# Moving the byte places of the streamed halves and of the low weights in a two-layer encoder

## The chip, the cores and the metric

The kernel runs on one core of one Trainium2 chip. The metric is the device time of one launch in microseconds; the kernel before takes 2561.47 us, the median of three runs (2561.24 to 2562.99). TensorE multiplies matrices: it holds a block of weights (the stationary operand) and streams the columns of the other operand past it, both read from SBUF, the on-chip memory, and adds into PSUM. VectorE and ScalarE do elementwise work, GpSimd a little, and SyncE's queue issues the loads of weights.

## The reference

A trunk of two layers over 272 tokens (16 learned tokens and 256 of input) of 2048 channels, in float32:

```python
for i in range(DEPTH):
    h = _rmsnorm(h_stream, norm_mix[i])
    proj = h @ w_in[i]                       # q, k, v, f, two gates
    ...                                      # attention: 8 heads over 2 key/value heads, rotary
    a_br = attn @ w_attn_br[i]
    ...                                      # fourier: real part of a 2-D DFT of f
    s_br = fr.reshape(B, L, FOURIER_WIDTH) @ w_four[i]
    merged = g_attn * a_br + g_four * s_br
    h_stream = h_stream + merged @ w_out[i]
    h2 = _rmsnorm(h_stream, norm_ffn[i])
    up = h2 @ w_up[i]                        # 2 x 5632 columns
    u_gate = _dwconv3_centred(up[..., :D_FF], w_conv[i], b_conv[i])
    u_val = up[..., D_FF:]
    h_stream = h_stream + (jax.nn.silu(u_gate) * u_val) @ w_down[i]
return h_stream[:, N_META:]
```

## The kernel before

Everything is kept transposed: channels on the 128 partitions, tokens along the row. A matrix product is done in three matmuls on numbers cut in two: a float32 value is a high half (the value rounded to the matmul's type, float32r) and a low half (what the rounding left). High weights times high half, high weights times low half and low weights times high half are added up in one PSUM tile; low times low is left out.

Weights come in chunks of 4 blocks of 128 rows by 256 columns (`CW` = 4, `MG` = 2). SyncE's queue loads a chunk into `raw`, ScalarE casts it into `wh` (L193), VectorE subtracts to get `wl` (L196); both are tiles of 4096 bytes a partition with three buffers each. A written list, `order`, gives the sequence of the groups of matmuls; `group` works through one of them. For each block of 128 rows and each of two output blocks it issues

```python
nc.tensor.matmul(o, h[:, c, sl], a, start=kt == 0, stop=False)    # L248: high weights, high half
nc.tensor.matmul(o, h[:, c, sl], b, start=False, stop=False)      # L249: high weights, low half
nc.tensor.matmul(o, lo[:, c, sl], a, start=False, stop=kt == nk - 1)  # L250: low weights, high half
```

or, where twice the width fits in a PSUM tile, the first two as one matmul over both halves (L244) and then the third (L245). Every matmul has its own weight load (LDWEIGHTS) ahead of it.

The groups are named f, k, v, q (inputs of the two branches), ga and gf (gates), s and a (branch outputs), o (the output product), ug and uv (the two halves of the up product) and d (the down product). f, k, v, q, ga, gf, ug and uv stream from `xHL`, which holds both halves of the scaled residual side by side; d streams from `gHL`; a from `qH` and `qL`; o from `mH` and `mL`. The row of each half has room for `XP` = 320 columns of 4 bytes (1280 bytes, five times 256), so that the 272 tokens can begin at a chosen column: `X_AT`, `Q_AT` and `G_AT` hold that column for layer 0 and layer 1.

Layer 0 works on all 272 tokens. Layer 1 drops columns whose results are not used: f, k and v take 272, then q, ga, gf, a, o and ug take 258 (from token 14) and uv and d take 256 (from token 16). There the two halves together fit 512 columns, so uv and d run as pairs of a 512 and a 256 column matmul; the last of d's groups runs as three of 256.

The order on each engine is the order in which the program is written; `split_w` is called a little ahead of its use by `pump`.

Of the kernel before, what the change touches and what calls it, by code (L numbers as in the profile page):

```python
# [10 lines left out]
F32 = mybir.dt.float32  # L11
F32R = mybir.dt.float32r
# [4 lines left out]
P = 128  # L17
# [3 lines left out]
T = NM + SEQ  # L21
# [3 lines left out]
NH = 8  # L25
# [7 lines left out]
CW = 4  # L33
MG = 2
FF_SPLIT = (24, 20)
PRE = 26
XP = 320
# [11 lines left out]
TH = T // 2 + 2  # L49
X_AT, Q_AT, G_AT = (8, 24), (24, 40), (40, 48)  # L50
BLK = ((0, 16), (16, 144), (144, 272))
# [60 lines left out]
def encoder_kernel(ctx, tc, xT, params, consts, bmat, w_in, w_abr, w_four, w_f64, w_out, w_up, w_down, outT):  # L112
# [7 lines left out]
    order = []  # L120
# [26 lines left out]
    chunks = [ch for _, chs in order for ch in chs]  # L147
    folded = {i for i, k in enumerate(k for k, chs in order for _ in chs) if k[1] == "s"}
    st = {"raw": 0, "fetch": 0, "next": 0, "grp": 0}
    raws, splits, behind = {}, {}, {}  # L150
# [36 lines left out]
    def split_w(i, a, b, eng=None):  # L187
        if i not in splits:
            splits[i] = tuple(wp.tile([P, CW, MG * P], F32R, tag=t, name=f"{t}{i}") for t in ("wh", "wl"))
        h, lo = splits[i]  # L190
        r = raws[i]
        if eng is None:
            nc.scalar.copy(h[:, a:b], r[:, a:b])  # L193
        else:
            eng.tensor_copy(h[:, a:b], r[:, a:b])
        nc.vector.tensor_tensor(lo[:, a:b], r[:, a:b], h[:, a:b].bitcast(F32), op=ALU.subtract)  # L196
        if b == CW:
            del raws[i]
# [187 lines left out]
    def xs(k, half, lo=0, l=0):  # L386
        return xHL[:, k, half, X_AT[l] + lo:X_AT[l] + T]

# [60 lines left out]
    for l in range(DEPTH):  # L449
# [7 lines left out]
        with tc.tile_pool(name=f"mix{l}", bufs=1) as mp:  # L457
            x64 = mp.tile([96, TH], F32R, name="x64")
            E = mp.tile([P, NH, XP], F32, tag="q1", name="E")[:, :, 0:T]
            qL = mp.tile([P, NH, XP], F32R, name="qL")[:, :, Q_AT[l]:Q_AT[l] + T]  # L460
            AHn = 3 * 4 * T
# [236 lines left out]
            for pn in pns:  # L698
                nc.gpsimd.memset(pn[:, 0:P], 0.0)
            qH = mp.tile([P, NH, XP], F32R, tag="q1", name="qH")[:, :, Q_AT[l]:Q_AT[l] + T]  # L700

# [149 lines left out]
            for half in range(2):  # L851
                mH = mL = None
                for kind, i in BRANCH_ORDER[half]:
# [19 lines left out]
                    else:  # L873
                        if mH is None:
                            drain()
                            mHf = mp.tile([P, AHn], F32R, tag="aH", name="mH")
                            mLf = mp.tile([P, ALn], F32R, tag="aL", name="mL")
                            mH, mL = (t_[:, :8 * XP].rearrange("p (k t) -> p k t", k=8)[:, :, Q_AT[l]:Q_AT[l] + T] for t_ in (mHf, mLf))
                        ps = group((l, "a", i), lambda kt: (qH[:, kt, lo:T], qL[:, kt, lo:T]), W)
# [16 lines left out]
        with tc.tile_pool(name=f"ffn{l}", bufs=1) as fp:  # L896
            hold = {}
            push(norm_stats(hold), 8)
            fused = 2 * W2 <= 512
            k0 = 0  # L900
            for c, n in enumerate(FF_SPLIT):
                gHL = fp.tile([P, FF_SPLIT[0], 2, XP], F32R, tag="gHL", name="gHL")[:, :, :, G_AT[l]:G_AT[l] + T]
                gH, gL = gHL[:, :, 0, :], gHL[:, :, 1, :]
                for i in range(k0 // MG, (k0 + n) // MG):
# [3 lines left out]
                    for m in range(MG):  # L908
# [12 lines left out]
                        cs.append(cv)  # L921
                    ps = group((l, "uv", i), (lambda kt: (xHL[:, kt, :, X_AT[l] + lo2:X_AT[l] + T],)) if fused else xr(lo2), W2)
                    for m in range(MG):
# [12 lines left out]
                for mg in range(8):  # L936
                    two = fused and not (lastc and mg == 7)
                    ps = group((l, "d", c, mg), (lambda kt: (gHL[:, kt, :, lo2:T],)) if two
                               else (lambda kt: (gH[:, kt, lo2:T], gL[:, kt, lo2:T])), W2)
# [64 lines left out]
```

## Time and profile before

| | |
|---|---|
| median of three runs | 2561.47 us |
| the profiled execution's own time | 2561.68 us |
| its span, first to last instruction | 2559.8 us |
| TensorE busy | 2552.6 us, 19732 matmuls |
| weight loads busy | 2494.2 us |
| VectorE, ScalarE busy | 1690.4 us, 1211.4 us |
| mean granted TensorE clock | 0.999 |

In the rows, PE is a matmul and PEld a weight load, DVE is VectorE, ACT is ScalarE. A row of the groups by shape gives the source line, the engine, output<-inputs by tile name, the shape, how many there were (x), then busy time and the mean duration of one in ns. Durations of successive matmuls overlap: one is shown some 280 ns long while the next begins some 120 ns after it began. A row of a window gives its limits, its length, then the busy time and count of each engine's instructions, and after these the granted clock, the share of the DMA engines and what they moved. A row of the timeline gives the start in us and the duration. A row of the waits gives the engine and line that waited, for whom, the total in us, the number of times and the longest.

### The profile page before, as it was taken

Reading aid. Unit: us, or ns where it says so; the run is one execution under the profiler, and the core shown is the slowest. Engines: PE = TensorE matmul, PEld = TensorE weight load, DVE = VectorE, ACT = ScalarE, POOL = GpSimd, SP = SyncE. Lnnn points to the kernel's source line nnn. Section 1 sums busy time; section 2 is a strip of 40 time slices with the busy share of each in tenths; the row PEclk is TensorE's granted clock in tenths of the full one; section 3 lists DMA queues with packets and bytes.
Section 4 is the critical chain, followed back from the end, with each engine's and each line's share of the span. In section 5 each row is a group of like instructions: output and inputs, shape, how many; then the busy total and the mean of one; then the engine's idle time right before and its main releaser. Section 6 shows DMA issues by size and latency. Waiting matters only on the chain.

```text
span 2559.8 us, 47859 instructions
## 1 busy us (share of the span) xinstructions
PE 2552.6 (100%) x19732; PEld 2494.2 (97%) x19732; DVE 1690.4 (66%) x2691; ACT 1211.4 (47%) x1741; POOL 18.3 (1%) x37
## 2 busy tenths in 40 slices
PE   9999999999999999999999999999999999999999
PEld 9999999999999999999999999999999998999988
DVE  7687767766565446655566878677766665566654
ACT  6455434554444334444444555345554543455443
POOL 0000000000000000000000000000000000000000
PEclk9999999999999999999999999999999999999999
DMA  7555656555555555555554546666555556655565
GB/s 236 166 153 166 192 183 189 185 175 179 180 176 181 177 178 181 175 181 178 177 172 153 174 150 199 192 199 191 184 186 189 185 187 190 189 188 186 186 202 160
DMA packets 132011, 465.34 MB, mean 182 GB/s; under 512 B 15312, under 2 KB 19280, under 8 KB 131792
## 3 DMA queue, kind: packets, MB, share of 16 engines
q1 hardware_dynamic: 127424, 457.37, 56.5%
q10 hardware_dynamic: 4368, 4.92, 0.6%
q8 instruction: 154, 2.52, 0.4%
q14 instruction: 65, 0.53, 0.1%
HBM read 457.35 MB, written 2.10 MB: 179 GB/s over the span
## 4 chain that ended last, share of the span: by engine, by line
PE 98%; DVE 1%; DMA 0%; ACT 0%; issue 0%; SPq 0%; DVEq 0%; ACTq 0%
PE ps_ug L249 7%; PE ps_ug L248 7%; PE ps_ug L250 7%; PE ps_uv L244 6%; PE ps_d L244 6%; PE ps_d L249 4%; PE ps_d L250 4%; PE ps_d L248 4%; PE ps_uv L248 3%; PE ps_uv L249 3%; PE ps_uv L250 3%; PE ps_uv L245 3%; PE ps_d L245 3%; PE ps_o L249 2%; PE ps_o L248 2%; PE ps_gf L248 2%
## 5 line engine op out<-in xcount | busy, mean ns | idle before, releaser
L196 DVE TENSOR_TENSOR wl<-raw,wh 128x1024 fp32r<-128x1024 f32 (+1 forms) x835 | 1016.8, 1220 | 697.3 <-ACT wh L193 692.4
L193 ACT CAST wh<-raw 128x1024 fp32r<-128x1024 f32 (+1 forms) x834 | 871.3, 1047 | 994.4 <-PE ps_ug L249 159.5
L248 PE MATMUL ps_ug<-xHL,wh 128*128 128x272 f32 (+1 forms) x1408 | 399.6, 284 | 0.0
L249 PE MATMUL ps_ug<-xHL,wh 128*128 128x272 f32 (+1 forms) x1408 | 399.0, 283 | 0.0
L250 PE MATMUL ps_ug<-xHL,wl 128*128 128x272 f32 (+1 forms) x1408 | 399.0, 283 | 0.0
L248 PEld LDWEIGHTS ps_ug<-xHL,wh 128*128 128x128 f32 x1408 | 264.2, 188 | 0.9
L249 PEld LDWEIGHTS ps_ug<-xHL,wh 128*128 128x128 f32 x1408 | 264.2, 188 | 0.1
L250 PEld LDWEIGHTS ps_ug<-xHL,wl 128*128 128x128 f32 x1408 | 264.1, 188 | 0.0
L244 PE MATMUL ps_uv<-xHL,wh 128*128 128x512 f32 x704 | 245.0, 390 | 0.0
L244 PE MATMUL ps_d<-gHL,wh 128*128 128x512 f32 x664 | 230.3, 391 | 0.0
L249 PE MATMUL ps_d<-gHL,wh 128*128 128x272 f32 (+1 forms) x744 | 212.0, 285 | 0.0
L248 PE MATMUL ps_d<-gHL,wh 128*128 128x272 f32 (+1 forms) x744 | 212.0, 285 | 0.0
L250 PE MATMUL ps_d<-gHL,wl 128*128 128x272 f32 (+1 forms) x744 | 212.0, 285 | 0.0
L248 PE MATMUL ps_uv<-xHL,wh 128*128 128x272 f32 x704 | 200.6, 285 | 0.0
L249 PE MATMUL ps_uv<-xHL,wh 128*128 128x272 f32 x704 | 200.6, 285 | 0.0
L250 PE MATMUL ps_uv<-xHL,wl 128*128 128x272 f32 x704 | 200.6, 285 | 0.0
L245 PE MATMUL ps_uv<-xHL,wl 128*128 128x256 f32 x704 | 198.5, 282 | 0.0
L245 PE MATMUL ps_d<-gHL,wl 128*128 128x256 f32 x664 | 185.9, 280 | 0.0
L244 PEld LDWEIGHTS ps_uv<-xHL,wh 128*128 128x128 f32 x704 | 132.1, 188 | 26.9
L244 PEld LDWEIGHTS ps_d<-gHL,wh 128*128 128x128 f32 x664 | 124.2, 187 | 27.2
L248 PE MATMUL ps_ga<-xHL,wh 128*128 128x272 f32 (+1 forms) x512 | 147.5, 288 | 0.0
L248 PE MATMUL ps_gf<-xHL,wh 128*128 128x272 f32 (+1 forms) x512 | 146.3, 286 | 0.0
(284 smaller groups left out, 5891.7 us busy)
## 6 DMA issues: line engine op xcount, KB each, us to landing
raw<-in_w_up SPq DMA_DIRECT2D x352, 512.0 KB, 3.5
raw<-in_w_in SPq DMA_DIRECT2D x207, 512.0 KB, 3.6
raw<-in_w_down SPq DMA_DIRECT2D x176, 512.0 KB, 3.5
raw<-in_w_out SPq DMA_DIRECT2D x64, 512.0 KB, 3.5
raw<-in_w_four SPq DMA_DIRECT2D x32, 512.0 KB, 3.7
raw<-in_w_abr SPq DMA_DIRECT2D x32, 512.0 KB, 3.5
qs<-qp ACTq DMA_DIRECT2D x32, 68.0 KB, 4.1
outT<-ot ACTq DMA_DIRECT2D x16, 128.0 KB, 4.0
```

Source lines behind the costliest of these rows:

```text
L193: nc.scalar.copy(h[:, a:b], r[:, a:b])
L196: nc.vector.tensor_tensor(lo[:, a:b], r[:, a:b], h[:, a:b].bitcast(F32), op=ALU.subtract)
L244: nc.tensor.matmul(o2, h[:, c, sl], ab, start=kt == 0, stop=False)
L245: nc.tensor.matmul(o, lo[:, c, sl], ab[:, 0, :], start=False, stop=kt == nk - 1)
L248: nc.tensor.matmul(o, h[:, c, sl], a, start=kt == 0, stop=False)
L249: nc.tensor.matmul(o, h[:, c, sl], b, start=False, stop=False)
L250: nc.tensor.matmul(o, lo[:, c, sl], a, start=False, stop=kt == nk - 1)
```

## The change

The change gives each half its own first column, and lets the low weights of a chunk begin at a place inside a longer tile (`WL_AT`, in columns of 4 bytes, by layer and kind of group; 0 where none is named). A tile of 32 columns that nothing uses (`shift`) moves the tiles behind it by 128 bytes. Where both halves are streamed by one matmul, the function `both` builds a view whose step between the halves is 320 columns plus the difference of the two places.

With the addresses that the built programs give to the tiles, the operands begin at these bytes, counted mod 256:

| groups | columns | high half | low half | high weights | low weights |
|---|---|---|---|---|---|
| layer 0: f, k, v, q, ga, gf, ug, uv, d | 272 | 32 -> 176 | 32 -> 48 | 128 | 128 -> 192 |
| layer 0: a, o | 272 | 32 -> 240 | 32 -> 80 | 128 | 128 -> 64 |
| layer 1: f, k, v | 272 | 96 | 96 -> 128 | 128 | 128 |
| layer 1: q, ga, gf, ug, a, o | 258 | 152 | 152 -> 184 | 128 | 128 |
| layer 1: uv | 512, 256 | 160 | 160 -> 192 | 128 | 128 -> 32 |
| layer 1: d | 512, 256 | 128 -> 0 | 128 -> 96 | 128 | 128 |

In the short description of the change, "258 columns at 232, 32, 0" is the fourth row: high weights less high half is 232 mod 256, low half less high half 32, low weights less high weights 0. The rows of every engine stand in the same order in both programs, with the same shapes and the same waits; only addresses and steps differ.

```diff
-X_AT, Q_AT, G_AT = (8, 24), (24, 40), (40, 48)
+X_AT, Q_AT, G_AT = ((44, 12), (24, 32)), ((44, 4), (8, 16)), ((12, 44), (16, 40))
+WL_AT = {(0, "a"): 48, (0, "o"): 48, (1, "uv"): 40}
+WL_AT.update({(0, k): 16 for k in ("q", "k", "v", "f", "f01", "ga", "gf", "ug", "uv", "d")})
...
+    wl_at = [WL_AT.get(k[:2], 0) for k, chs in order for _ in chs]
...
     def split_w(i, a, b, eng=None):
         if i not in splits:
-            splits[i] = tuple(wp.tile([P, CW, MG * P], F32R, tag=t, name=f"{t}{i}") for t in ("wh", "wl"))
+            h = wp.tile([P, CW, MG * P], F32R, tag="wh", name=f"wh{i}")
+            lo = wp.tile([P, CW * MG * P + 64], F32R, tag="wl", name=f"wl{i}")
+            o = wl_at[i]
+            splits[i] = h, lo[:, o:o + CW * MG * P].rearrange("p (c m) -> p c m", c=CW)
...
     def xs(k, half, lo=0, l=0):
-        return xHL[:, k, half, X_AT[l] + lo:X_AT[l] + T]
+        return xHL[:, k, half, X_AT[l][half] + lo:X_AT[l][half] + T]
...
             x64 = mp.tile([96, TH], F32R, name="x64")
+            mp.tile([P, 32], F32, name="shift")
             E = mp.tile([P, NH, XP], F32, tag="q1", name="E")[:, :, 0:T]
-            qL = mp.tile([P, NH, XP], F32R, name="qL")[:, :, Q_AT[l]:Q_AT[l] + T]
+            qL = mp.tile([P, NH, XP], F32R, name="qL")[:, :, Q_AT[l][1]:Q_AT[l][1] + T]
...
-            qH = mp.tile([P, NH, XP], F32R, tag="q1", name="qH")[:, :, Q_AT[l]:Q_AT[l] + T]
+            qH = mp.tile([P, NH, XP], F32R, tag="q1", name="qH")[:, :, Q_AT[l][0]:Q_AT[l][0] + T]
...
+            def both(t_, k, at):
+                a, n = at[0] + lo2, XP + at[1] - at[0]
+                if n == XP:
+                    return t_[:, k, :, a:a + W2]
+                b = 2 * XP * k + a
+                s = min(b, 2 * XP * t_.shape[1] - 2 * n)
+                return t_.rearrange("p k r n -> p (k r n)")[:, s:s + 2 * n].rearrange("p (r n) -> p r n", r=2)[:, :, b - s:b - s + W2]
...
-                gHL = fp.tile([P, FF_SPLIT[0], 2, XP], F32R, tag="gHL", name="gHL")[:, :, :, G_AT[l]:G_AT[l] + T]
-                gH, gL = gHL[:, :, 0, :], gHL[:, :, 1, :]
+                gHL = fp.tile([P, FF_SPLIT[0], 2, XP], F32R, tag="gHL", name="gHL")
+                gH, gL = (gHL[:, :, e, G_AT[l][e]:G_AT[l][e] + T] for e in range(2))
...
-                    ps = group((l, "uv", i), (lambda kt: (xHL[:, kt, :, X_AT[l] + lo2:X_AT[l] + T],)) if fused else xr(lo2), W2)
+                    ps = group((l, "uv", i), (lambda kt: (both(xHL, kt, X_AT[l]),)) if fused else xr(lo2), W2)
...
-                    ps = group((l, "d", c, mg), (lambda kt: (gHL[:, kt, :, lo2:T],)) if two
+                    ps = group((l, "d", c, mg), (lambda kt: (both(gHL, kt, G_AT[l]),)) if two
```

More of the change, by code (lines that the diff above doesn't have):

```diff
@@ L877, in encoder_kernel @@
                             mLf = mp.tile([P, ALn], F32R, tag="aL", name="mL")
-                            mH, mL = (t_[:, :8 * XP].rearrange("p (k t) -> p k t", k=8)[:, :, Q_AT[l]:Q_AT[l] + T] for t_ in (mHf, mLf))
+                            mH, mL = (t_[:, :8 * XP].rearrange("p (k t) -> p k t", k=8)[:, :, o:o + T] for t_, o in zip((mHf, mLf), Q_AT[l]))
                         ps = group((l, "a", i), lambda kt: (qH[:, kt, lo:T], qL[:, kt, lo:T]), W)
```

## The prediction

> **What bounds the kernel now.** I read the head of the page first, then the chain that ended last, then what TensorE waited for, then the groups by shape, and last windows inside single stages, because a rate per matmul has to be read where only one kind of matmul runs.
>
> ```profile
> span 2559.8 us, 47859 instructions
> PE 2552.6 (100%) x19732; PEld 2494.2 (97%) x19732; DVE 1690.4 (66%) x2691; ACT 1211.4 (47%) x1741; POOL 18.3 (1%) x37
> ...
> PE 98%; DVE 1%; DMA 0%; ACT 0%; issue 0%; SPq 0%; DVEq 0%; ACTq 0%
> ...
> L196 DVE TENSOR_TENSOR wl<-raw,wh 128x1024 fp32r<-128x1024 f32 (+1 forms) x835 | 1016.8, 1220 | 697.3 <-ACT wh L193 692.4
> L193 ACT CAST wh<-raw 128x1024 fp32r<-128x1024 f32 (+1 forms) x834 | 871.3, 1047 | 994.4 <-PE ps_ug L249 159.5
> ```
>
> TensorE is busy from end to end and carries 98% of the chain. The longest total that it waited for anything is short:
>
> ```profile
> PE ps_f L304 <- ACT wh L193: 1.8, 2, 0.9
> ```
>
> So nothing but the time from one matmul's start to the next (the pitch, below) can move the span by more than a few us. The shown duration of a matmul does not give it, since each overlaps the next. I take it from windows that lie inside one kind of work: the window's length divided by the count beside PE, less the two or so that began before the window opens.
>
> ```profile
> 560.00:660.00 100.00, 100.00 (x813) 100.00 (x813) 61.92 (x86) 46.66 (x61) 0.00 (x0) 1.00 0.57 180
> 815.00:950.00 135.00, 135.00 (x1097) 135.00 (x1096) 61.84 (x60) 47.89 (x46) 0.00 (x0) 1.00 0.57 179
> 322.00:366.00 44.00, 44.00 (x359) 44.00 (x358) 27.03 (x35) 15.30 (x16) 0.00 (x0) 1.00 0.61 191
> 1311.00:1356.00 45.00, 45.00 (x361) 44.92 (x360) 26.75 (x57) 17.17 (x25) 0.85 (x1) 1.00 0.54 164
> 1616.00:1660.00 44.00, 44.00 (x373) 44.00 (x372) 27.61 (x37) 16.74 (x18) 0.00 (x0) 1.00 0.59 192
> 1860.00:1871.00 11.00, 11.00 (x94) 11.00 (x93) 6.66 (x9) 4.72 (x8) 0.00 (x0) 1.00 0.65 192
> 2090.00:2210.00 120.00, 120.00 (x694) 105.77 (x694) 64.20 (x73) 45.36 (x43) 0.00 (x0) 1.00 0.61 191
> ```
>
> The first three are layer 0, all 272 columns: ug with uv, d, and o. They give 100/811, 135/1095 and 44/357, all 123.3 ns. The fourth is f of layer 1, also 272 columns, but with both operands 64 bytes further on: 45/359 = 125.4 ns. The fifth and sixth are 258 columns in layer 1 at one and the same place, o and ug: 44/371 = 118.6 and 11/91.7 = 120.0 ns. The last is d of layer 1, pairs of a 512 and a 256 column matmul: 120/346 = 346.8 ns a pair. The granted clock is 1.00 in all of them. So the place of the operands is worth 2 ns in 123, and one place can have two rates, 1.3 ns apart.
>
> How much could a better place win at most? These rows bound it.
>
> ```profile
> 75.41 0.28 PE L545 MATMUL ps_fb<-BL,o1H 128*128 128x138 f32 x1
> 75.52 0.28 PE L546 MATMUL ps_fb<-BH,o1L 128*128 128x138 f32 x1
> ...
> 76.08 0.28 PE L547 MATMUL ps_fb<-br,o1r 128*128 128x138 f32 x1
> ```
>
> ```profile
> 1899.89 0.39 PE L244 MATMUL ps_uv<-xHL,wh 128*128 128x512 f32 x1
> 1900.12 0.28 PE L245 MATMUL ps_uv<-xHL,wl 128*128 128x256 f32 x1
> 1900.23 0.39 PE L244 MATMUL ps_uv<-xHL,wh 128*128 128x512 f32 x1
> ...
> 1900.93 0.39 PE L244 MATMUL ps_uv<-xHL,wh 128*128 128x512 f32 x1
> ```
>
> Six steps of 138-column matmuls take 0.67 us: 112 ns each although they stream half as much as a 272-column one, so 112 ns is what one weight load costs by itself. A 512-column matmul holds the engine 230 ns, a 256-column one 117 ns (three pairs in 1.04 us): 256 further columns cost 113 ns, 0.443 ns a column. By that estimate 272 columns would need 120.5 ns, 258 columns 114.3, a pair of 768 columns 340. The difference to the windows, about 2.9, 4 to 6 and 6.8 ns, is what the place can still win.
>
> **Why a place could matter.** The next weights are read while a matmul streams:
>
> ```profile
> 1860.11 0.28 PE L250 MATMUL ps_ug<-xHL,wl 128*128 128x258 f32 x1
> 1860.12 0.19 PEld L248 LDWEIGHTS ps_ug<-xHL,wh 128*128 128x128 f32 x1
> 1860.23 0.28 PE L248 MATMUL ps_ug<-xHL,wh 128*128 128x258 f32 x1
> 1860.23 0.19 PEld L249 LDWEIGHTS ps_ug<-xHL,wh 128*128 128x128 f32 x1
> ```
>
> Both begin within 10 ns. An estimate from the rows above: the stream reads 4 bytes per 0.443 ns, 9.0 bytes a ns; a load reads 512 bytes in 112 ns, 4.6 a ns. The stream gains 4.4 bytes a ns on the load, a lap of 256 bytes in 58 ns. If reads that stand at the same byte of 256 get in each other's way (my assumption; the layer-1 f window speaks for a place mod 256, not for why), the meetings come at D/4.4 ns and 58 ns later, D being the place of the weights loaded less the place of the half streamed. While the high half streams against high weights, wh is loaded next, then with the low half streaming wl, then with the high half wh. Before, D is the same for all three. At D = 96 (layer 0) the meetings are at 22 and 80 ns: two. At D = 32 (layer 1, f) at 7, 65 and 123: the third still falls on the matmul. Then 2.9/2 and 4.9/3 both make about 1.5 ns a meeting. At D = 232 (258 columns) they are at 53 and 111 ns, and the load ends at about 112: a meeting on the edge fits a place with two rates.
>
> **The change, part by part.** No instruction, wait, shape or DMA is added, removed or moved. What changes is D.
>
> Counts come from the groups by shape; each row is one of three lines with the same count:
>
> ```profile
> L249 PE MATMUL ps_ug<-xHL,wh 128*128 128x272 f32 x704 | 200.6, 285 | 0.0
> L249 PE MATMUL ps_uv<-xHL,wh 128*128 128x272 f32 x704 | 200.6, 285 | 0.0
> L249 PE MATMUL ps_d<-gHL,wh 128*128 128x272 f32 x704 | 200.6, 285 | 0.0
> L249 PE MATMUL ps_ga<-xHL,wh 128*128 128x272 f32 x256 | 73.2, 286 | 0.0
> L249 PE MATMUL ps_o<-mL,wh 128*128 128x272 f32 x256 | 73.0, 285 | 0.0
> L249 PE MATMUL ps_a<-qL,wh 128*128 128x272 f32 x128 | 36.5, 285 | 0.0
> L249 PE MATMUL ps_ug<-xHL,wh 128*128 128x258 f32 x704 | 198.4, 282 | 0.0
> L244 PE MATMUL ps_uv<-xHL,wh 128*128 128x512 f32 x704 | 245.0, 390 | 0.0
> L244 PE MATMUL ps_d<-gHL,wh 128*128 128x512 f32 x664 | 230.3, 391 | 0.0
> ```
>
> 1. Layer 0, everything streamed from xHL and gHL: 3 x (704 + 704 + 704 + 256 for ga, as many for gf, half as many for q, 192 for f, k and v) = 8832 matmuls. D goes from 96, 96, 96 to 208, 144, 208. Meetings at 47 and 105, 33 and 90, 47 and 105 ns. The late one falls into the last 7 ns of a load, where little is left to disturb. I price this as one meeting less in each matmul, 1.45 ns: 8832 x 1.45 = -12.8 us. Ends: all of the 2.9 ns won, -25.6 us; or the pitch of the worst 272-column row, 125.4 in place of 123.3, +18.5 us. I take the middle of the gain because both of its ends need every meeting to behave alike.
>
> 2. Layer 0, a and o: 3 x (128 + 256) = 1152 matmuls, D to 144, 240, 144; only the middle one is near the end (112 ns). A third of a meeting: 1152 x 0.5 = -0.6 us; ends -3.3 and +2.4.
>
> 3. Layer 1, 258 columns: ug 3 x 704 = 2112, and ga, gf, o, q, a 3 x 1024 = 3072. The high half stays at D = 232, the low half's loads go to 200, meetings at 45 and 103 ns, off the edge. One odd distance in three is enough to throw a stream out of the slower of two rates, so I let ug go to the 118.6 of o: 2112 x 1.3 = -2.7 us, and leave the others, mostly there, at 0. Ends: down to the 114.3 of columns alone, 5184 x 4.6 = -24 us; or all at 120.0, 3072 x 1.3 = +4 us.
>
> 4. Layer 1, f, k, v (192 a line, 576): D of one load in three goes from 32 to 0. -0.4 us, ends -2.8 and +1.
>
> 5. Pairs of 512 and 256 columns: the one load under the 512 columns goes from D = 224 (uv) and 0 (d) to 128, the other stays at 224 (uv) or goes from 0 to 128 (d). D = 0 meets at 0, 58 and 116 ns, D = 128 at 29 and 87. One meeting less in each load of d, 664 x 2 x 1.5 = -2.0, and one load in two for uv at half that, -0.5. Ends: the whole 6.8 ns, 1368 x 6.8 = -9.3 us; or +3. The 120 unpaired matmuls of the last group are left out.
>
> 6. Writes at other places: the casts and subtractions of the weights (1047 and 1220 ns) and of the activations. A chunk of weights feeds 24 matmuls, 24 x 123.3 ns = 2.96 us, so the subtraction could take twice as long before TensorE saw it. 0; without that cover 835 subtractions a tenth slower would be 100 us.
>
> Sum: -12.8 - 0.6 - 2.7 - 0.4 - 2.5 = -19 us. The profiled execution took 2561.7 us (span 2559.8), 0.2 above the median 2561.5 of the three runs. Forecast: 2561.5 - 19 = 2542.5 us.
>
> **Rivals.**
> *Slower.* The layer-0 distances are worse than 96. In the window of f a place costs 2.1 ns, and nothing in the trace shows D = 208 or 144 with weights at another place than the high ones. Place: layer 0's 9984 matmuls; price up to +2.1 x 9984 = +21 us, less about 6 won in layer 1: 2577 us. It decides once the 272-column pitch passes 123.9 ns, for 0.6 x 9984 eats the 6 us. Against it: no new load stands at 32, the one distance known to be slow.
>
> *Nothing changes.* The extra nanoseconds belong to the column count and the change of weights, not to the place: 2561. The three layer-0 windows agree to 0.1 ns whatever tile they read, which speaks for it; but their places are equal too, and f's window at another place speaks against. [...]
>
> *Nearly all is won.* Every place loses its meetings: -25.6 - 3.3 - 24 - 9.3 = -62, about 2500 us. Against it: 258 columns never held a steady pitch under 118.6 in any window.
>
> **How the numbers follow.** The forecast or something like it 0.55 (2520 to 2555); nearly all won 0.10; nothing changes 0.10; slower 0.25. A measurement of this kernel tells 0.2%, 5 us, from no change. Faster 0.65, same 0.10, slower 0.25. The forecast's own range is 2520 to 2555. For 8 in 10 the range takes in the no-change case and most of the slower one, up to 2580, and reaches down to 2502, which leaves out about half of the largest gain.
>
> **What would show it.** The windows of layer 0 should read about 822 in place of 813 matmuls in 100 us at 121.9 ns; a count of 805 or less is the slower rival. ug in layer 1 should pass 95 matmuls in 11 us, like o. The pairs of d should fall from 346.8 to near 344 ns. Durations and idle times of DVE and ACT should not move. The forecast is wrong if the place acts by something else than the distance between the two reads, above all if moving the low weights alone sets off a rate that no row here shows.

## The result, and the profile after

| | before | after |
|---|---|---|
| median | 2562.18 us (4 runs) | 2542.73 us (4 runs, 2541.63 to 2544.20) |
| ratio of the two, 95% interval | | 0.9925 (0.9907 to 0.9942) |
| span of the profiled execution | 2559.8 us | 2539.8 us |

The forecast was 2542.5 us. The time came out at it; most of the reasons for it did not hold, and that is what the runs below are about.

The head of the page after the change, the chain that ended last, and the two groups that write the split weights:

```profile
span 2539.8 us, 47859 instructions
PE 2532.2 (100%) x19732; PEld 2472.8 (97%) x19732; DVE 1690.7 (67%) x2691; ACT 1210.0 (48%) x1741; POOL 18.3 (1%) x37
...
PE 98%; DVE 1%; ACT 0%; DMA 0%; issue 0%; SPq 0%; DVEq 0%; ACTq 0%
...
L202 DVE TENSOR_TENSOR wl<-raw,wh 128x1024 fp32r<-128x1024 f32 (+1 forms) x835 | 1017.1, 1221 | 680.7 <-ACT wh L199 675.2
L199 ACT CAST wh<-raw 128x1024 fp32r<-128x1024 f32 (+1 forms) x834 | 870.1, 1045 | 971.2 <-PE ps_ug L255 160.8
```

TensorE lost 20.4 us of busy time and the span 20.0, with the same 19732 matmuls. It still carries 98% of the chain. The subtraction takes 1221 ns (1220 before), the cast 1045 (1047): the writes to other places cost nothing that these rows show.

The windows that answer to those before, in the same order (layer 0 ug with uv, d, o; then layer 1 f, o, ug, pairs of d). The lines of the three matmuls are now L254 to L256, those of a pair L250 and L251.

```profile
560.00:660.00 100.00, 100.00 (x820) 100.00 (x819) 62.93 (x88) 47.15 (x62) 0.00 (x0) 1.00 0.52 180
820.00:920.00 100.00, 100.00 (x821) 100.00 (x820) 46.42 (x46) 35.67 (x34) 0.00 (x0) 1.00 0.52 179
322.00:365.00 43.00, 43.00 (x355) 43.00 (x353) 25.40 (x33) 15.62 (x15) 0.00 (x0) 1.00 0.57 184
1298.00:1342.00 44.00, 44.00 (x357) 43.92 (x356) 27.54 (x57) 17.94 (x25) 1.87 (x5) 1.00 0.46 163
1605.00:1645.00 40.00, 40.00 (x342) 40.00 (x342) 24.68 (x34) 14.74 (x14) 0.00 (x0) 1.00 0.58 198
1868.40:1879.40 11.00, 11.00 (x96) 11.00 (x95) 6.86 (x10) 5.01 (x7) 0.00 (x0) 1.00 0.55 192
2075.00:2195.00 120.00, 120.00 (x701) 106.17 (x701) 63.69 (x74) 46.09 (x44) 0.00 (x0) 1.00 0.55 190
```

Counted as in the prediction (two less than the count beside PE): 100/818 = 122.2 ns in layer 0 where it was 123.3; o of layer 1 40/340 = 117.6 where it was 118.6; ug 11/94 = 117.0 where it was 120.0; a pair of d 120/349.5 = 343.3 where it was 346.8. The granted clock is 1.00 in all of them.

The windows are short and their ends cost a tenth or two of a ns. From here on I also use sums over the whole trace: the time from the start of each matmul to the start of the next, added up by kind of group. "For three" means such a sum over one matmul each of high weights with high half, high weights with low half, and low weights with high half, while the group runs steadily: the mean time from a start to the third start after it, without the few that a wait lengthens by 20 ns or more. With these sums the 20.0 us come from:

| | forecast | measured |
|---|---|---|
| layer 0, streamed from xHL and gHL | -12.8 | -9.4 |
| layer 0, a and o | -0.6 | -1.3 |
| layer 1, 258 columns | -2.7 | -7.4 (ug -4.3) |
| layer 1, f, k, v | -0.4 | -0.8 |
| pairs, d and uv | -2.5 | -2.2 (d -2.5, uv +0.3) |
| all else (s +1.0; the first two groups of f, which have lines of their own, +0.2) | 0 | +1.2 |
| sum | -19.0 | -19.9 |

Three matmuls of layer 0 now take 366.7 ns (123.3 + 121.7 + 121.7) where most groups took 370.0; three of 258 columns take 353.3 where they took 356.0 or 360.0.

### The profile page after: what moved, and what is told of

It reads as the page before. It is cut to its first block, busy times and chain, and to the rows that moved or that the text cites. A ratio compares the mean times of both kernels' runs of the same rounds, so it can differ in the third digit from the quotient of the medians.

```text
span 2539.8 us, 47859 instructions
## 1 busy us (share of the span) xinstructions
PE 2532.2 (100%) x19732; PEld 2472.8 (97%) x19732; DVE 1690.7 (67%) x2691; ACT 1210.0 (48%) x1741; POOL 18.3 (1%) x37
## 4 chain that ended last, share of the span: by engine, by line
PE 98%; DVE 1%; ACT 0%; DMA 0%; issue 0%; SPq 0%; DVEq 0%; ACTq 0%
PE ps_ug L254 7%; PE ps_ug L255 7%; PE ps_ug L256 7%; PE ps_uv L250 6%; PE ps_d L250 6%; PE ps_d L256 4%; PE ps_d L254 4%; PE ps_d L255 4%; PE ps_uv L254 3%; PE ps_uv L256 3%; PE ps_uv L255 3%; PE ps_uv L251 3%; PE ps_d L251 3%; PE ps_o L254 2%; PE ps_gf L254 2%; PE ps_o L255 2%
## 5 line engine op out<-in xcount | busy, mean ns | idle before, releaser
L202 DVE TENSOR_TENSOR wl<-raw,wh 128x1024 fp32r<-128x1024 f32 (+1 forms) x835 | 1017.1, 1221 | 680.7 <-ACT wh L199 675.2
L199 ACT CAST wh<-raw 128x1024 fp32r<-128x1024 f32 (+1 forms) x834 | 870.1, 1045 | 971.2 <-PE ps_ug L255 160.8
L254 PE MATMUL ps_ug<-xHL,wh 128*128 128x272 f32 (+1 forms) x1408 | 400.8, 285 | 0.0
L256 PE MATMUL ps_ug<-xHL,wl 128*128 128x272 f32 (+1 forms) x1408 | 396.3, 281 | 0.0
L254 PEld LDWEIGHTS ps_ug<-xHL,wh 128*128 128x128 f32 x1408 | 264.3, 188 | 0.9
L256 PEld LDWEIGHTS ps_ug<-xHL,wl 128*128 128x128 f32 x1408 | 264.3, 188 | 0.0
L250 PE MATMUL ps_uv<-xHL,wh 128*128 128x512 f32 x704 | 245.4, 393 | 0.0
L250 PE MATMUL ps_d<-gHL,wh 128*128 128x512 f32 x664 | 228.1, 390 | 0.0
L254 PE MATMUL ps_d<-gHL,wh 128*128 128x272 f32 (+1 forms) x744 | 212.5, 286 | 0.0
L256 PE MATMUL ps_d<-gHL,wl 128*128 128x272 f32 (+1 forms) x744 | 211.9, 285 | 0.0
L254 PE MATMUL ps_uv<-xHL,wh 128*128 128x272 f32 x704 | 201.4, 286 | 0.0
L256 PE MATMUL ps_uv<-xHL,wl 128*128 128x272 f32 x704 | 200.7, 285 | 0.0
L251 PE MATMUL ps_uv<-xHL,wl 128*128 128x256 f32 x704 | 197.1, 280 | 0.0
L251 PE MATMUL ps_d<-gHL,wl 128*128 128x256 f32 x664 | 184.9, 279 | 0.0
L250 PEld LDWEIGHTS ps_uv<-xHL,wh 128*128 128x128 f32 x704 | 132.2, 188 | 28.5
L250 PEld LDWEIGHTS ps_d<-gHL,wh 128*128 128x128 f32 x664 | 124.6, 188 | 26.3
L254 PE MATMUL ps_ga<-xHL,wh 128*128 128x272 f32 (+1 forms) x512 | 147.7, 289 | 0.0
L254 PE MATMUL ps_gf<-xHL,wh 128*128 128x272 f32 (+1 forms) x512 | 146.8, 287 | 0.0
```

The lines of the kernel that those rows point to most:

```text
L250: nc.tensor.matmul(o2, h[:, c, sl], ab, start=kt == 0, stop=False)
L251: nc.tensor.matmul(o, lo[:, c, sl], ab[:, 0, :], start=False, stop=kt == nk - 1)
```

## The experiments

All kernels compute the whole reference; they differ only in the bytes at which operands begin, and some have weight tiles longer by 256 bytes, which alone leaves every place mod 256 as it was. My theory was that of the prediction: a matmul's rate is set by the distance, mod 256, from the half that streams to the weights that are loaded meanwhile.

**The halves alone.** The change with the low weights left at 128.

```diff
-WL_AT = {(0, "a"): 48, (0, "o"): 48, (1, "uv"): 40}
-WL_AT.update({(0, k): 16 for k in ("q", "k", "v", "f", "f01", "ga", "gf", "ug", "uv", "d")})
+WL_AT = {}
```

> The halves moved as in the change, the low weights left where they were. The theory of distances says that only the distance D from the streamed half to the weights loaded under it counts, in the order of the three loads: layer 0 from xHL and gHL (208, 80, 208), a and o (144, 48, 144), layer 1 at 258 columns as in the change (232, 200, 232), f, k, v likewise, uv back at 224, 224. So the 258-column groups must read 117.8 ns as in the changed kernel, f, k and v 124.6, and layer 0 must keep most of its gain, since two of its three distances stay: about 122 to 122.8 ns; in all 12 to 17 us faster than the kernel before (2545 to 2550). The rival, that the low weights' own place carries the gain of layer 0, says 123.3 ns or more there and about 8 us faster in all (2554), all of it in layer 1.

**The low weights alone.** The kernel before, with nothing but `WL_AT` and the longer tile for the low weights.

```diff
 X_AT, Q_AT, G_AT = (8, 24), (24, 40), (40, 48)
+WL_AT = {(0, "a"): 48, (0, "o"): 48, (1, "uv"): 40}
+WL_AT.update({(0, k): 16 for k in ("q", "k", "v", "f", "f01", "ga", "gf", "ug", "uv", "d")})
```

> The low weights moved as in the change, the halves left. Distances: layer 0 from xHL and gHL (96, 160, 96), a and o (96, 32, 96), 258 columns as before (232, 232, 232), uv (128 under the 512 columns, 224 under the 256). The theory of distances says: 258 columns unchanged at 118.6 to 120.0 ns, a and o of layer 0 slower than 123.3 by about a third of the 2.1 ns that the distance 32 costs in layer 1, layer 0 otherwise within 0.7 ns of 123.3 either way; in all within 6 us of the kernel before. The rival of the low weights' own place says that layer 0 takes the changed kernel's 122.2 ns: 10 us faster (2552).

Measured: the halves alone 2564.6 us, ratio 1.0011 (1.0002 to 1.0020); the low weights alone 2571.7 us, ratio 1.0038 (1.0024 to 1.0051). Windows of layer 0 (ug with uv, then d), layer 1 o and pairs of d, first for the halves alone, then for the low weights alone:

```profile
560.00:660.00 100.00, 100.00 (x806) 100.00 (x805) 59.96 (x82) 44.48 (x58) 0.00 (x0) 1.00 0.55 177
820.00:920.00 100.00, 100.00 (x805) 100.00 (x805) 45.21 (x45) 34.85 (x34) 0.00 (x0) 1.00 0.55 176
1626.00:1666.00 40.00, 40.00 (x342) 40.00 (x341) 24.70 (x33) 14.75 (x14) 0.00 (x0) 1.00 0.62 199
2095.00:2215.00 120.00, 120.00 (x701) 106.18 (x700) 64.69 (x75) 46.38 (x45) 0.00 (x0) 1.00 0.61 191
```

```profile
560.00:660.00 100.00, 100.00 (x806) 100.00 (x805) 59.41 (x82) 45.43 (x58) 0.00 (x0) 1.00 0.56 175
820.00:920.00 100.00, 100.00 (x806) 100.00 (x805) 44.63 (x44) 35.65 (x34) 0.00 (x0) 1.00 0.57 176
1622.00:1662.00 40.00, 40.00 (x336) 40.00 (x335) 24.17 (x33) 15.57 (x18) 0.00 (x0) 1.00 0.58 185
2095.00:2215.00 120.00, 120.00 (x695) 105.80 (x694) 65.53 (x78) 47.06 (x48) 0.00 (x0) 1.00 0.61 190
```

Layer 1's gain comes from the halves alone: 342 matmuls of o and 701 of d, as in the change, and -7.6 us in the 258 columns, -2.6 in d by the sums. In layer 0 each part alone is slower than before (806 against 813 matmuls; +9.0 us and +9.3 us in what streams from xHL and gHL), and the two together are faster (820; -9.4 us). So the parts don't add. By meetings counted for each matmul, a gain of either part in its own matmul would have shown.

The low weights alone show one thing more. In this kernel the four operands of the 258 columns begin at the same bytes mod 256 as before, and still their rates are others. The first eight groups of o take 360.0 ns for three where they took 356.0, the last eight 356.0 as before, and 20 of the 22 groups of ug take 356.0 where all but the first took 360.0, which is 2.5 us. A window of ug (94 matmuls before), then one of the second half of o, to be held against the 336 of the first half above:

```profile
1894.20:1905.20 11.00, 11.00 (x95) 11.00 (x94) 6.79 (x10) 5.05 (x7) 0.00 (x0) 1.00 0.62 191
1779.00:1819.00 40.00, 40.00 (x340) 40.00 (x339) 33.09 (x57) 24.19 (x40) 0.00 (x0) 1.00 0.62 186
```

So the place mod 256 alone does not fix the rate. What ran before may count, or a place counted to a larger unit, since the longer tiles move others by whole multiples of 256 bytes; these runs do not tell which.

**All half-to-weights distances kept.** The kernel before, with the low half and the low weights both 32 bytes further back in every group: high weights less high half and low weights less low half stay as they were, only the low operands stand elsewhere against the high ones. (In the pairs the low weights are loaded under a stream that begins with the high half, so there one distance does change.)

```diff
-X_AT, Q_AT, G_AT = (8, 24), (24, 40), (40, 48)
+X_AT, Q_AT, G_AT = ((8, 0), (24, 16)), ((24, 16), (40, 32)), ((40, 32), (48, 40))
...
+    wl_at = [(0 if k[1] == "s" else 56) for k, chs in order for _ in chs]
```

> The kernel before, with the low half and the low weights both 32 bytes further back, everything else where it was. Each half streams against the weights loaded under it at the old distance: layer 0 (96, 96, 96), 258 columns (232, 232, 232), f, k, v (32, 32, 32); only the pairs of uv and d change, for their one low load runs under the 512 columns that begin with the high half. Theory, only the distance of the half streamed to the weights loaded under it counts: layer 0 at 123.3 ns as before, 258 columns at 118.6 or 120.0 as before, the whole within 6 us of the kernel before. Rival, the place of the low operands relative to the high ones counts (low half less high half, low weights less high weights, as the short description of the change has it): other pitches, 1 ns or more away, and a time off by 8 us or more.

Measured: 2583.4 us, ratio 1.0085 (1.0068 to 1.0102). Layer 0 is 13.9 us slower than before by the sums:

```profile
560.00:660.00 100.00, 100.00 (x801) 100.00 (x800) 59.99 (x82) 44.42 (x57) 0.00 (x0) 1.00 0.55 176
820.00:920.00 100.00, 100.00 (x801) 100.00 (x800) 45.42 (x47) 35.75 (x35) 0.00 (x0) 1.00 0.55 175
```

100/799 = 125.2 ns with the distances that gave 123.3. The distance from half to weights isn't what sets the rate, not alone. Of the rest of the loss, 7.4 us lie in the pairs. The 258 columns come out level by the sums (-0.1 us), but at other rates: 357.4 to 358.6 ns for three in place of 356.0 and 360.0.

**Scans.** Five kernels give each group of ug, uv, d and some of the gates a place of its own, 8 or 16 bytes from the last, with both halves where the kernel before has them. In the first, both weights move together; in the second only the low ones; in the other three both move, with the low ones 64 or 32 bytes before, or 96 behind, the high ones. The first one:

```diff
+def scan_step(k):
+    l, kind, i = k[0], k[1], k[-1]
+    if kind == "ug":
+        return 2 * i
+    if kind == "uv":
+        return (2 * i + 44) % 64 if l == 0 else 2 * i
+    if kind == "d":
+        i += 8 * k[2]
+        return (4 * i) % 64 if l == 0 else (2 * i + 32) % 64
+    if l == 1 and kind in ("ga", "gf"):
+        return (2 * i + (44 if kind == "ga" else 60)) % 64
+    return 0
+
+def w_place(k):
+    return scan_step(k), scan_step(k)
...
-            splits[i] = tuple(wp.tile([P, CW, MG * P], F32R, tag=t, name=f"{t}{i}") for t in ("wh", "wl"))
+            hf = wp.tile([P, CW * MG * P + 64], F32R, tag="wh", name=f"wh{i}")
+            lf = wp.tile([P, CW * MG * P + 64], F32R, tag="wl", name=f"wl{i}")
+            splits[i] = tuple(t[:, o:o + CW * MG * P].rearrange("p (c m) -> p c m", c=CW) for t, o in zip((hf, lf), w_at[i]))
```

The others differ in `w_place` alone: `0, scan_step(k)` in the second, and `s, (s - 16) % 64`, `s, (s - 8) % 64`, `s, (s + 24) % 64` in the last three.

> The kernel before, but each group of ug, uv and d (and ga, gf in layer 1) has its high and low weights begin 8 bytes (d of layer 0: 16) further on than the group before, so that one run shows the steady pitch at 32 places, with one and the same distance for all three loads. The theory of distances with meetings that cost 1.5 ns each says: a pitch of 272 columns near 126 ns for distances from about 0 to 40, where three meetings fall on a matmul, near 123.3 elsewhere, and lower, 121 to 122, at about 200 to 224, where the second meeting falls into the last ns of the load. The rival, that not the distance but the place of the weights in their own row counts, would show no such single region, but a pattern that repeats every 64 bytes or less. That nothing depends on the place would be 123.3 throughout. The time as a whole: 2555 to 2590 us.

> The same scan with the low weights alone, so that the first and third distance stay as before and the second runs through all places. The theory of distances says: a third of the rise and fall of the scan with both weights, so 272 columns between 122.6 and 124.3 ns. The rival that the low weights' own place counts says the full range of the other scan. The time as a whole: 2555 to 2570 us.

> Both halves where the kernel before has them, equal places; in the groups of ug, uv and d the high weights run through the 32 places again, and the low weights begin 64 bytes before them. At the group with D = 208 the three distances are 208, 144, 208, as in the change's layer 0, but with no half moved. Theory of distances: the three matmuls there take 366.7 ns together, the change's pitch of 122.2, and no place with equal distances (the first scan) has that. Rival, the offset between the halves is needed: nothing under 370 ns at that group. The time as a whole 2560 to 2585 us.

> The same with the low weights 32 bytes before the high ones. In layer 1 at D = 232 the distances are 232, 200, 232, as the change has them for 258 columns. Theory of distances: 353.3 ns for three matmuls there (the change's 117.8); the rival: 356 or 360 as in the kernel before. The time as a whole 2560 to 2585 us.

> The same with the low weights 96 bytes after the high ones. At D = 144 in layer 0 the distances are 144, 240, 144, as the change has them for a and o. Theory of distances: 366.7 ns for three matmuls there; the rival: 370 or more. The time as a whole 2560 to 2585 us.

Measured, in one run each, with the sums for three of ug, uv and d of layer 0 (60 groups a kernel) and of the 258 columns:

| scan | time, us | 272 columns: least, mean, most | 258 columns: least |
|---|---|---|---|
| both together | 2581.6 | 370.0, 376.7, 383.5 | 353.3 |
| low weights alone | 2574.1 | 370.0 (unmoved), 375.5, 386.5 | 353.4 |
| low 64 before | 2578.7 | 373.3, 375.9, 380.1 | 346.6 |
| low 32 before | 2578.4 | 373.3, 376.1, 380.0 | 353.3 |
| low 96 behind | 2579.9 | 370.0, 377.1, 389.8 | 346.6 |

Three things follow. First, none of the 300 groups of layer 0 reached the change's 366.7, also not the two that stood at the change's distances 208 and 144 with both halves at one place (373.3 and 373.4, in the scan with the low weights 64 before). The three groups at the change's distances of a and o (low 96 behind) took 380.0. The first scan answers the theory by itself: at distances of 200 to 224, where it expected the lowest pitch, 121 to 122 ns, the six groups took 377.1 to 380.0 for three, 125.7 to 126.7 each. The mean of all places is 375 to 377, so the kernel before, at 370, already had a good one. Second, the sums gather on steps of 6.67 ns: 346.7, 353.3, 360.0, 366.7, 373.3 and 380.0 are 52 to 57 of them, the 370.0 of the kernel before 111 in two threes, its 356.0 267 in five. Of the 360 groups of ug, uv and d of layer 0 in the scans (with the one further down), 173 lie within 0.35 ns of a whole number of steps and 69 of a half, where an even spread would give 38 each. That looks like a few repeating patterns, not like small disturbances that add up. Third, one place can have two of them. In the first scan two or three groups of layer 0 stand at each of 21 places; at 15 they agree within 0.5 ns, at 6 they do not. For one of the six: ug's group 9 and uv's group 19 of layer 0 stand at the same bytes (both halves 32, both weights 200) and stream the same columns, yet one takes 380.0 and the other 370.0:

```profile
744.50:754.50 10.00, 10.00 (x82) 10.00 (x81) 4.72 (x6) 3.74 (x5) 0.00 (x0) 1.00 0.58 178
1143.00:1153.00 10.00, 10.00 (x84) 10.00 (x83) 6.71 (x10) 4.84 (x7) 0.00 (x0) 1.00 0.60 197
```

The widest step is in layer 1 of the scan with the low weights 64 before. Halves at 152, high weights at 16 and low weights at 208, then, 8 bytes on, 24 and 216:

```profile
2369.80:2379.80 10.00, 10.00 (x89) 10.00 (x88) 6.26 (x9) 4.46 (x7) 0.00 (x0) 1.00 0.63 203
2392.20:2402.20 10.00, 10.00 (x74) 10.00 (x73) 5.11 (x7) 3.98 (x7) 0.00 (x0) 1.00 0.52 161
```

346.6 against 420.0 ns for three. The slow ones show in the timeline as starts 0.14 us apart:

```profile
2392.25 0.31 PE L270 MATMUL ps_ug<-xHL,wh 128*128 128x258 f32 x1
2392.39 0.31 PE L271 MATMUL ps_ug<-xHL,wh 128*128 128x258 f32 x1
2392.53 0.31 PE L272 MATMUL ps_ug<-xHL,wl 128*128 128x258 f32 x1
2392.67 0.31 PE L270 MATMUL ps_ug<-xHL,wh 128*128 128x258 f32 x1
```

**All four operands 16 bytes up.** If not the distance from half to weights, then perhaps the distances among all four. This kernel keeps every one of them:

```diff
-X_AT, Q_AT, G_AT = ((44, 12), (24, 32)), ((44, 4), (8, 16)), ((12, 44), (16, 40))
+X_AT, Q_AT, G_AT = ((48, 16), (28, 36)), ((48, 8), (12, 20)), ((16, 48), (20, 44))
...
+def w_place(k):
+    return (0, 0) if k[1] == "s" else (4, 4 + WL_AT.get(k[:2], 0))
```

> The change with every operand of its three-matmul and pair groups moved 16 bytes up, both halves and both weights alike, so that every distance among the four stays. If only the distances set the rate, layer 0 keeps 122.2 ns, the 258 columns 117.8 and the pairs of d 343.5, and the time is the change's, 2542.7 within 3 us. If the place itself counts, layer 0 goes to what it has at an average place, 124 to 126 ns, and the time to 2560 to 2585.

Measured: 2582.5 us, ratio 1.0082 (1.0065 to 1.0099).

```profile
560.00:660.00 100.00, 100.00 (x792) 100.00 (x791) 59.18 (x81) 44.21 (x57) 0.00 (x0) 1.00 0.55 173
820.00:920.00 100.00, 100.00 (x792) 100.00 (x791) 45.87 (x47) 35.27 (x35) 0.00 (x0) 1.00 0.53 174
1640.00:1680.00 40.00, 40.00 (x342) 40.00 (x341) 24.70 (x33) 14.83 (x15) 0.00 (x0) 1.00 0.63 200
2107.00:2227.00 120.00, 120.00 (x687) 105.18 (x687) 64.57 (x75) 45.62 (x46) 0.00 (x0) 1.00 0.58 189
```

Layer 0 goes from 122.2 to 100/790 = 126.6 ns (380.0 for three in ug, uv and d; a and o take 373.3), 34 us above the change in what streams from xHL and gHL, with every distance as in it; pairs of d go from 343.3 to 350.4. The 258 columns keep their 342 matmuls in 40 us, though the three intervals change places among themselves (120.0, 118.3, 115.0 in the change; 114, 120, 119 here). The longer weight tiles are not the cause: the scan below has them too, and its groups of o in layer 0, left at the change's places, keep 366.7. So the place itself counts, not only distances. Where the unit lies to which it is counted, these runs don't tell: one shift of 16 bytes was tried.

**A scan inside the change.** The halves stay as in the change. In layer 0, ug and uv move the low weights alone, d moves both with 64 bytes between them; in layer 1 both move, the low ones 64 before.

```diff
+def w_place(k):
+    l, kind, i = k[0], k[1], k[-1]
+    if l == 0 and kind in ("ug", "uv"):
+        return 0, (16 + 2 * i + (0 if kind == "ug" else 44)) % 64
+    if l == 0 and kind == "d":
+        n = 4 * (i + 8 * k[2]) % 64
+        return n, (n + 16) % 64
+    if l == 1 and kind in ("ug", "ga", "gf"):
+        n = (2 * i + {"ug": 0, "ga": 44, "gf": 60}[kind]) % 64
+        return n, (n + 48) % 64
+    return 0, WL_AT.get((l, kind), 0)
```

> The change with its halves left where they are, and a place of its own for each group. In layer 0 ug and uv move the low weights alone by 8 bytes a group: if the change's place is one good place among many, some groups reach 366.7 ns for three again and most lie between 370 and 380; if 366.7 is a floor (816 columns in 366.7 ns and 774 in 346.6 are 2.23 columns per ns both), none goes lower. The d groups of layer 0 move both weights by 16 bytes a group and keep their 64 bytes between: by the distances from half to weights alone only the unmoved one has 366.7. In layer 1 the 258 columns, with their low half 32 bytes behind the high one, have the low weights 64 bytes before the high ones and both moved by 8 bytes a group: 346.6 at 2 or 3 of 32 places again, none lower, if it is a floor there. The whole: 2560 to 2585 us, since most places are worse than the change's.

Measured: 2561.5 us in one run. Of the 32 places of the low weights, three give 366.7 ns for three: the change's 192, 112 and 216. Eight bytes to either side of 192 there are 376.6 and 373.4. Of the other 15 places of d, one gives 366.7, 112 and 176 for high and low weights. Nothing is lower. In the 258 columns, with the low half 32 behind the high one, nothing is under 353.4, though three of these pairs of weight places had 346.6 with the halves together. The change's place of layer 0 is one of a few, with worse neighbours, and what suits the weights depends on where the halves are.

**Two versions from the scans.** The first takes for all 258 columns of layer 1 a place that showed 346.6 ns for three in two groups of a scan: halves both at 152, high weights 144, low weights 80. It also moves uv's low weights and f, k and v to their best places in the scans.

```diff
-X_AT, Q_AT, G_AT = ((44, 12), (24, 32)), ((44, 4), (8, 16)), ((12, 44), (16, 40))
+X_AT, Q_AT, G_AT = ((44, 12), (24, 24)), ((44, 4), (8, 8)), ((12, 44), (16, 40))
...
+def w_place(k):
+    l, kind = k[:2]
+    if l == 1 and kind in ("q", "ga", "gf", "ug", "a", "o"):
+        return 4, 52
+    if l == 1 and kind == "uv":
+        return 0, 8
+    if l == 1 and kind in ("f", "f01", "k", "v"):
+        return 38, 38
+    return 0, WL_AT.get((l, kind), 0)
```

> The change's layer 0 and its places for d of layer 1, with other places in the rest of layer 1: the halves of the 258 columns both at 152, their high weights at 144 and low weights at 80 (three matmuls in 346.6 ns in the run with the low weights 64 bytes before the high ones, against 353.3 in the change); the low weights of uv pairs at the place of the half streamed, its high weights 32 bytes before it (344.6 ns a pair in the scan of the low weights, 347.1 in the change); f, k and v 184 bytes behind the halves. If all four places relative to each other set a steady rate that a whole group keeps, 5184 matmuls lose 2.2 ns each, 11.6 us, and the uv pairs 704 times 2.5 ns, 1.8 us: 2529 us, with 95 to 96 ug matmuls in 11 us. If the rates of the scans were accidents of where each group began (two groups at one place had different rates there), the 258 columns come out between 353 and 360 ns for three and the run within 2537 to 2555.

Measured: 2538.4 us, ratio 0.9909 (0.9894 to 0.9924); the interval overlaps that of the change. By the sums uv gains 1.9 us on the change, f, k and v 0.5, the 258 columns only 0.4 of the 11.6. Two windows of o say why, its first half and its second:

```profile
1605.00:1645.00 40.00, 40.00 (x349) 40.00 (x348) 25.41 (x34) 14.77 (x15) 0.00 (x0) 1.00 0.62 204
1758.00:1798.00 40.00, 40.00 (x335) 40.00 (x335) 32.13 (x56) 24.29 (x41) 0.00 (x0) 1.00 0.57 184
```

Same program line, same bytes, same columns: 40/347 = 115.3 ns and 40/333 = 120.1 ns. The place has two rates, 346.6 and 360.0 for three, and which one a group has goes over to the next: of the groups from a 4 to the end of o all are at 360.0, the 8 of o ahead of them all at 346.6. The change's 258 columns show 353.3 in every group but a few that wait at their start. That one rate lies between the two, and over the whole of the 258 columns the two come out level with it.

The second version keeps 144 and 80 for ug, where 20 of 22 groups had 346.6, and takes for the others the remaining places that a scan had shown at 346.6.

```diff
-    if l == 1 and kind in ("q", "ga", "gf", "ug", "a", "o"):
-        return 4, 52
...
+    if l == 0:
+        return 0, WL_AT.get((l, kind), 0)
+    return {"q": (36, 20), "a": (36, 20), "o": (58, 42), "ga": (38, 62), "gf": (38, 62), "ug": (4, 52), "uv": (0, 8),
+            "f": (38, 38), "f01": (38, 38), "k": (38, 38), "v": (38, 38)}.get(kind, (0, 0))
```

> The run before it (layer 1 at 144 and 80) with other places for the 258 columns outside ug: high and low weights at 16 and 208 for q and a, at 104 and 40 for o, at 24 and 120 for ga and gf, the halves at 152 as there. Each of these had 346.6 ns for three in the one or two groups of a scan that stood at it. At 144 and 80 the same four places gave 346.6 in 28 groups or so and 360.0 in the rest of the 258 columns, a rate that went over from one group to the next. If each place has two rates and the one before a group decides, some of these kinds show 346.6 and some 353 to 366, and the time stays within 3 us of 2538.4. If these places have the one rate seen in the scans, the 3072 matmuls outside ug lose about 3 ns each, and the time is 2529 to 2532.

Measured: 2533.5 us, ratio 0.9890 (0.9873 to 0.9906), the lowest median of all; its span is 7.8 us under the change's, 5.5 of it in the 258 columns. The two halves of o:

```profile
1605.00:1645.00 40.00, 40.00 (x348) 40.00 (x348) 25.41 (x35) 14.75 (x14) 0.00 (x0) 1.00 0.62 200
1755.00:1795.00 40.00, 40.00 (x349) 40.00 (x347) 33.67 (x58) 25.50 (x43) 0.00 (x0) 1.00 0.60 191
```

All 16 groups of o are at 346.6 now, and so are the gates from gf 2 on. The place of q and a (16 and 208) has two rates again: two of q's four groups at 360.0, two near 346.6, and all eight of a at 360.0. So the time came out between the two expectations: some of these places have one rate, at least in this program, and some two.

## Why the prediction was right in its time and wrong in its reason

- *TensorE's pitch is all that can move the span.* Right: busy time fell by 20.4 us, the span by 20.0, and TensorE keeps 98% of the chain.
- *What a place costs, from the window of f: 125.4 ns, 2.1 more.* Read too low. That window also holds 29 other matmuls, 24 of them with 65 columns:

```profile
L248 PE MATMUL ps_f<-xHL,wh 128*128 128x272 f32 x110 | 32.4, 294 | 0.0
L499 PE MATMUL ps_fa<-cst,E 128*128 128x65 f32 x12 | 2.3, 275 | 0.0
L498 PE MATMUL ps_fa<-cst,E 128*128 128x65 f32 x12 | 2.2, 261 | 0.0
```

  The 272-column matmuls in it follow each other at 127.5 ns, waits included, and where f runs steadily three take 376.0 to 380.0, 125.3 to 126.7 each. So that place cost 2.0 to 3.3 ns and had two rates itself, and one of the two numbers behind the 1.5 ns a meeting was too small.
- *The meetings, at D/4.4 ns and 58 ns later.* Wrong. It is the step on which all terms rested. With the same D in every matmul, layer 0 went to 125.2 ns (low half and low weights moved together). With the distances among all four operands kept as well, it went to 126.6 (all four 16 bytes up). And each part of the change alone is slower in layer 0 while both together are faster; a count of meetings in each matmul by itself can't give that. In its place the runs show steady rates of the whole sequence of three, gathered on steps of 6.67 ns, chosen by the places of all four operands, and at some places by something more, perhaps what ran before.
- *Step 1, layer 0.* -12.8 forecast, -9.4 measured. 1.45 ns for a meeting less, in every matmul, was too much: the mean fell by 1.1 ns, and not evenly. The high half under high weights stayed at 123.3; the other two fell to 121.7.
- *Step 2, a and o.* -0.6 forecast, -1.3 measured: the three reach 366.7 too.
- *Step 3, 258 columns.* -2.7 forecast, -7.4 measured. The step that failed is to leave q, ga, gf, a and o at 0 because they were "mostly there" at 118.6. That was a rate of the old place, not a floor; the new place has a rate of its own, 117.8 ns, and all of them took it, ug with -4.3 and the others with -3.1. That "one odd distance in three" throws the stream out of the slower of two rates was an assumption that no row of before shows, and it came true in the result only (353.3 ns for three where ug had 360.0): with the low weights alone moved, 20 of the 22 groups of ug left 360.0 for 356.0 though none of their distances changed.
- *Step 4, f, k, v* -0.4 forecast, -0.8 measured. *Step 5, pairs* -2.5 forecast, -2.2 measured: d fell by 2.5 us against 2.0 forecast, uv rose by 0.3 against a fall of 0.5. *Step 6, writes:* 0, and the durations of both groups are within 2 ns.
- *The sum.* -19 against -20.0 in the profiled execution. Step 1 was 3.4 too large and step 3 was 4.7 too small, so they nearly cancelled. A forecast right to a fifth of a microsecond says little of its reason here.
- *The rivals.* The slower one was real though not at these places: with D = 96 kept in layer 0 but the low operands at other places it is 2583, and 2564.6 and 2571.7 with one part alone. Nothing changes: by that the place should not matter; it did, with 366.7 ns for three 272-column matmuls in the change and 380.0 with all four operands 16 bytes up, at a granted clock of 1.00 in both. Why it does, no run here shows. Nearly all won, 2500: not reached, and no place of any run went under 122.2 ns a matmul for 272 columns and 115.5 for 258, where the estimate from columns alone said 120.5 and 114.3.
- *What would show it.* 820 matmuls for the 822 foretold, 96 of ug in 11 us for 95, 343.3 ns for 344. These signs came, and not one of them could tell the meetings from another rule of places. The idle times of DVE and ACT, which were not to move, fell with the span (before the subtractions from 697.3 to 680.7 us, before the casts from 994.4 to 971.2). The sign of being wrong that the prediction named above all others came as well: with the low weights alone moved, layer 0 went to 100/804 = 124.4 ns, a rate that none of its rows had. What ruled the meetings out were that run, the first scan and the runs with the distances kept.

What stays open is the rule itself: to which unit the place counts, why these steps, and what picks one of two rates at the same place mod 256.

## What to carry to other kernels

Where every matmul has its own weight load and TensorE is never idle, measure the pitch in windows by kind of group, and try the operands' byte places together: here two parts that lost 9.0 and 9.3 us in layer 0 alone won 9.4 together, and 8 bytes to either side of a place with 366.7 ns for three stood 376.6 and 373.4. Prefer a place that shows one rate over many groups (353.3 in the 258 columns of the change) to one with a lower rate in a group or two (144 and 80: 346.6 in the scan, 346.6 and 360.0 in use), and test it where it is to stand, behind the same neighbours. And when a sum of estimated terms hits the total, check the terms; hold fixed what your mechanism says matters, and see whether the time stays.

## What the runs showed of the hardware

- Three matmuls with 272 columns, each with its weight load, took 366.7 ns (the change) to 389.8 (the scan with the low weights 96 behind) by the byte places of the four operands, with 258 columns 346.6 to 420.0 (both in the scan with them 64 before), at a granted clock of 1.00; the mean over the places scanned is 375.5 to 377.1 for 272 columns.
- Steady sums gather on steps of 6.67 ns: 52 to 57 of them for three, and 63 at the slowest place. In layer 0, 242 of the 360 scanned groups lie within 0.35 ns of a whole or half number of steps.
- One place had two steady rates within one run (346.6 and 360.0 for 258 columns at 144 and 80, 370.0 and 380.0 for 272 in the first scan), and at 144 and 80 a rate went over from a group to the next (360.0 in all groups from a 4 to the end of o). Between the kernel before and the one with the low weights alone moved, it changed at operands that stand at the same bytes mod 256 in both (356.0 and 360.0 in the first eight groups of o).
- The lowest rates found are all about 2.23 columns a ns: 816 columns in 366.7 ns, 774 in 346.6, 768 in 343.3. That this is a limit was not shown; no place tried went past it.
